# Two weight sums of a seven-product FFN on GpSimd, and three plain column pairs in place of four

## The chip, the cores and the metric

The kernel runs on one core of one Trainium2 chip. The metric is the device time of one execution in microseconds. The engines of the core are TensorE (PE, matmuls; PEld is its weight load), VectorE (DVE), ScalarE (ACT), GpSimd (POOL) and SyncE (SP). SP issues most of the DMA transfers, GpSimd those that add into their target. Each engine takes its instructions in the order in which they were written into its queue, and waits where an operand or a buffer isn't ready.

## The reference

A decoder trunk of two layers on 512 tokens of width 1024, all in float32. Each layer is an FFN, a token mixer and another FFN; the mixer of the first layer is a short gated convolution, that of the second is native sparse attention (NSA). Before each of the six a root mean square norm is scaled and shifted by a conditioning vector. So there are four FFNs; the change touches the last three. One FFN is:

```python
def swiglu(h, w_in, w_out):
    g, u = jnp.split(h @ w_in, 2, axis=-1)
    return (jax.nn.silu(g) * u) @ w_out
```

`h` is 512 x 1024, `w_in` 1024 x 5632 (gate and up, 2816 columns each), `w_out` 2816 x 1024.

## The kernel before

**Precision.** A float32 matmul is made of three matmuls in the format fp32r. An operand is split (L176, L177): ScalarE copies it to the high half, VectorE subtracts that from the operand for the low half. `mm3` (L185 to L187) multiplies high by high, high by low and low by high into the same PSUM tile. `weights` (L189 to L202) loads a block of weights into a tile `wraw` (L196, three buffers) and splits it into `whi` and `wlo` (three buffers each).

**Stages.** In the trace the first FFN and the convolution take the time up to about 569 us, the second FFN lies from there to about 904, the third to 1243, NSA to 1590 and the fourth, the last, to the end. The first FFN has code of its own (`ffn_first`), the other three run `ffn`, with f = 1, 2, 3.

**An FFN in `ffn`.** The 2816 columns of gate and up are 22 blocks of 128, numbered j. For each j the hidden block 128 x 512 (columns by tokens) is silu(gate) * up, kept split as `ahi`, `alo`. There are two ways to make gate and up of a block:

- A plain pair: gate and up, each as 8 blocks of the contraction by 3 matmuls for each half of the tokens (128x256 outputs), so 2 x 8 x 3 x 2 = 96 matmuls of 128x256, or half as many of 128x512.
- `seven_products` (L507 to L563): gate and up weights of the block are taken as the rows and the two halves of the contraction as the columns of a 2x2 matrix, the activations (halves of the contraction by halves of the tokens) as another, and the four results come from seven products instead of eight. Each product has 4 blocks of the contraction by 3 matmuls, so a block takes 7 x 4 x 3 = 84 matmuls of 128x256. The activations enter as quarters, four of them as sums that `quarters` makes once per FFN (their halves are `th`, `tl`). The weights enter as a11, a12 (`raw`, L525, split to `whi`, `wlo`), a22 (L526, its own tile `a22`), two differences s3, s1 in `qa` and two sums s2, s4 in `qb`. `qa` is loaded by SP (L520, L521, 128x512 each) and a DMA of GpSimd then accumulates onto it (L523, waits for both). `qb` is made by two additions of 128x512 (L527, L528) from `qa` and `raw`. Split halves: `qah`, `qal` of `qa`; `qbh`, `qbl` of a22 (128x512) and of `qb` (128x1024).

The seven products run in the order a11, a12, s3, s1, a22, s2, s4. The results are put together by VectorE (L556 to L562) and split into `ahi`, `alo`. Two products of one column block share a PSUM tile, three such tiles are used per block.

**The order of blocks.** Blocks 0 and 1 are plain pairs made while the norm is finished (`head_start`), block 2 is a plain pair whose gate weights are loaded into a place of their own, block 3 is a plain pair, and the other 18 are `seven_products`. The output projection is done in four parts, as soon as the hidden blocks of a part are there: `FOUR = ((0, 6), (6, 12), (12, 18), (18, 22))` (L31, L592). So in the first group two blocks by seven products precede the first output part, then six, six and four.

**Buffers of `qa`.** The first three come from two buffers of their own, then four places are cycled: the tiles of the activations' quarter that only plain pairs read (`hhi1`, `hlo1`), and the two own buffers (`sums`, L580 on). A quarter place can be loaded once the last plain pair has read it; the third `qa` once the first block's `qa` has been read (by its split and by L527). `raw`, `whi`, `wlo` have three buffers each, `a22` shares four buffers with other temporaries (`tmp`), `qb` has one.

**What sets the order.** The source is written block by block, and a scheduler in the framework places each instruction into its engine's queue by its own estimate of when its operands are ready, so a load of a later block may stand before or behind loads of an earlier one. The queues that result are fixed at compile time.

Of the kernel before, what the change touches and what calls it, by code (L numbers as in the profile page):

```python
# [17 lines left out]
ALU = mybir.AluOpType  # L18
# [36 lines left out]
def decoder_kernel(ctx, tc, xT, cT, ng, adaw, adab, ffi, ffo, cwi, cw, cwo,  # L55
                   nwi, nwg, pos, w1, w2, qg, kg, nwo, rb, onehot, rowok, out):
    nc = tc.nc
# [20 lines left out]
    def psum(name, tag="mm"):  # L78
        tag = next(six) if tag == "mm" else {"pr": "o"}.get(tag, tag)
        return ps.tile([P, T], F32, name=name, tag=tag, bufs=2)  # L80
# [4 lines left out]
    def tmp(name, n=T, tag="t"):  # L85
        bufs, size = TAGS[tag]
        return tp.tile([P, n], F32, name=name, tag=tag, padded_shape=[P, size], bufs=bufs)
# [87 lines left out]
    def split(src, hi, lo):  # L175
        nc.scalar.activation(hi, src, AF.Copy)  # L176
        nc.vector.tensor_tensor(lo, src, hi, ALU.subtract)  # L177
# [6 lines left out]
    def mm3(o, sh, sl, mh, ml, first, last):  # L184
        nc.tensor.matmul(o, sh, mh, start=first, stop=False)  # L185
        nc.tensor.matmul(o, sh, ml, start=False, stop=False)  # L186
        nc.tensor.matmul(o, sl, mh, start=False, stop=last)  # L187
# [16 lines left out]
    def project(o, w, wc, h, ks, first, last, a=0, b=T):  # L204
        c = slice(wc * P, (wc + 1) * P)
        for n, (kw, k) in enumerate(ks):
            mm3(o, w[0][:, kw, c], w[1][:, kw, c], h[0][k][:, a:b], h[1][k][:, a:b],
                first and n == 0, last and n == len(ks) - 1)
# [194 lines left out]
    def ffn_in(f, j, c, own=None):  # L403
        return weights(ffi[f, j, c], KD, P, own)
# [6 lines left out]
    class Hidden:  # L411
# [4 lines left out]
        def keep(self, af):  # L416
            hi = self.fa.tile([P, T], F32R, name="ahi", tag="a")
            lo = self.fa.tile([P, T], F32R, name="alo", tag="a")
            split(af, hi, lo)
            self.hi.append(hi)  # L420
            self.lo.append(lo)
# [21 lines left out]
    def pair(f, j, h, own=None, gate=None, halves=False):  # L443
        gu = []
        for c in range(2):
            w = gate if gate and not c else ffn_in(f, j, c, own if c else None)
            o = psum("gu")
            for a, b in HALVES if gate or halves else ((0, T),):
                project(o[:, a:b], w, 0, h, [(k, k) for k in range(KD)], True, True, a, b)
            gu.append(o)  # L450
        return gu
# [47 lines left out]
    def ffn(s, f, nrm, nxt, w0, ahead):  # L499
        with ExitStack() as es:  # L500
            hp = pool(es, "hp", 1)
            hid = Hidden(es, 12)
            keep = hid.keep
            nj = 2
# [3 lines left out]
            def seven_products(j):  # L508
                QT = KD * P // 2
                quart = lambda c, k: ffi[f, j, c].rearrange("p k n -> p (k n)")[:, k * QT:(k + 1) * QT]  # L510
                raw = wp.tile([P, 2, QT], F32, name="wraw", tag="wraw", bufs=3)
                whi = wp.tile([P, 2, QT], F32R, name="whi", tag="whi", bufs=3)
                wlo = wp.tile([P, 2, QT], F32R, name="wlo", tag="wlo", bufs=3)
                qa = next(sums)()
                a22 = tmp("a22")
                qb = swa.tile([P, 2, QT], F32, name="qb")
                ah_, al_ = (sw.tile([P, 2, QT], F32R, name=f"qa{e}", bufs=2) for e in "hl")
                bh_, bl_ = (sw.tile([P, 3, QT], F32R, name=f"qb{e}") for e in "hl")
                e = sw.tile([P, 4, HT], F32, name="e")
                nc.sync.dma_start(qa[:, 0], quart(0, 0))  # L520
                nc.sync.dma_start(qa[:, 1], quart(1, 1))  # L521
                a21 = quart(1, 0)
                nc.gpsimd.dma_start(qa, bass.AP(tensor=a21.tensor, offset=a21.offset, ap=[a21.ap[0], [0, 2], a21.ap[1]]),  # L523
                                    accum_op=ALU.add)
                nc.sync.dma_start(raw.rearrange("p a b -> p (a b)"), ffi[f, j, 0].rearrange("p k n -> p (k n)"))  # L525
                nc.sync.dma_start(a22, quart(1, 1))  # L526
                nc.vector.tensor_tensor(qb[:, 0], qa[:, 1], raw[:, 0], ALU.add)  # L527
                nc.vector.tensor_tensor(qb[:, 1], qb[:, 0], raw[:, 1], ALU.add)  # L528
                split(raw, whi, wlo)
                split(qa, ah_, al_)  # L530
                split(a22, bh_[:, 0], bl_[:, 0])
                split(qb, bh_[:, 1:3], bl_[:, 1:3])

                def product(o, w, b):
                    for i in range(KD // 2):
                        c = slice(i * P, (i + 1) * P)
                        mh, ml = b(i)
                        mm3(o, w[0][:, c], w[1][:, c], mh, ml, i == 0, i == KD // 2 - 1)

                a11, a12 = [(whi[:, i], wlo[:, i]) for i in range(2)]  # L540
                s3, s1 = [(ah_[:, i], al_[:, i]) for i in range(2)]
                a22, s2, s4 = [(bh_[:, i], bl_[:, i]) for i in range(3)]
                t1, t2, t3, t4 = nrm.blocks
                lo, hi = slice(0, HT), slice(HT, T)
                ox, oy, oz = psum("gu"), psum("gu"), psum("gu")
                both = lambda o: o.rearrange("p (a b) -> p a b", a=2)
                product(oy[:, lo], a11, nrm.quarter(0, 0))
                p1 = tmp("p1", HT, "xr")
                with tc.high_priority():
                    nc.scalar.activation(p1, oy[:, lo], AF.Copy)  # L550
                product(ox[:, lo], a12, nrm.quarter(1, 0))
                product(oy[:, hi], s3, t3)
                product(oy[:, lo], s1, t1)
                product(oz[:, hi], a22, t4)
                product(ox[:, hi], s2, t2)
                nc.vector.tensor_tensor(e[:, 0:2], both(ox), p1[:, None].to_broadcast([P, 2, HT]), ALU.add)  # L556
                nc.vector.tensor_tensor(e[:, 2], oy[:, hi], e[:, 1], ALU.add)
                nc.vector.tensor_tensor(e[:, 1:4:2], oy[:, None, lo].to_broadcast([P, 2, HT]), e[:, 1:3], ALU.add)
                product(oz[:, lo], s4, nrm.quarter(1, 1))
                nc.vector.tensor_tensor(e[:, 1:3], both(oz), e[:, 1:3], ALU.add)  # L560
                nc.scalar.activation(e[:, 0:2], e[:, 0:2], AF.Silu)
                nc.vector.scalar_tensor_tensor(e[:, 0:2], e[:, 0:2], -1.0, e[:, 2:4], op0=ALU.mult, op1=ALU.mult)  # L562
                keep(e[:, 0:2].rearrange("p a b -> p (a b)"))  # L563
# [5 lines left out]
            with ExitStack() as tf_es:  # L569
                nrm.alloc_seven(hp, pool(tf_es, "tf", 1))  # L570
                h = nrm.hi, nrm.lo
# [15 lines left out]
            shift(sw, 64)  # L587
            for j in range(nj + 1):
                hid.activate(os[2 * j], os[2 * j + 1])
            hid.activate(*pair(f, nj + 1, h, halves=True))  # L590
            nj += 2
            for p, (j0, j1) in enumerate(FOUR):  # L592
                for j in range(max(j0, nj), j1):
                    seven_products(j)
                n = j1 - j0
                a = (hid.hi[j0:j1], hid.lo[j0:j1])
                if p < len(FOUR) - 1:
                    outputs(range(KD), lambda d: ffn_out(f, d, 1, j0, j1), a, n,
                            lambda d, o: nc.vector.scalar_tensor_tensor(x[d], o, mod(s, 2, d), x[d], op0=ALU.mult, op1=ALU.add))  # L599
# [4 lines left out]
            for i, d in enumerate(range(0, KD, 2)):  # L604
                if i < 2:
                    ws.append(ffn_out(f, d, 2, j0, j1))
                else:
                    t = (2, 0)[i - 2]
                    to = [tt.tile([P, KD // 2, HT], F32R, name=f"t{e}{t}").rearrange("p a b -> p (a b)") for e in "hl"]
                    raw = swa.tile([P, 2, KD * P // 2], F32, name="qa", bufs=2).rearrange("p a b -> p (a b)")  # L610
# [660 lines left out]
    ada_es.close()  # L1271
    nrm, nxt = nxt, Norm(3)
    w = ffn(2, 1, nrm, nxt, w, ffn_ahead(2))
    nrm, nxt = nxt, Norm(4)
    w = ffn(3, 2, nrm, nxt, w, lambda: nsa_in(4))
    nrm, nxt = nxt, Norm(5)
    w = nsa(4, nrm, nxt, w, ffn_ahead(3))
    ffn(5, 3, nxt, None, w, None)


# [73 lines left out]
```

## Time and profile before

| what | value |
|---|---|
| median of 3 runs | 1951.38 us (1949.58 to 1952.29) |
| profiled execution | 1950.53 us |
| its span, first to last instruction | 1948.8 us |
| mean granted TensorE clock | 0.999 |
| second FFN, 569 to 904 us | PE busy 334.94, VectorE 251.91, GpSimd 24.08 |
| third FFN, 904 to 1243 us | PE busy 338.77, VectorE 257.55, GpSimd 22.84 |
| NSA, 1243 to 1590 us | PE busy 329.08, VectorE 278.57, GpSimd 109.56 |
| last FFN, 1590 to 1949 us | PE busy 351.52, VectorE 256.07, GpSimd 19.25 |
| first block by seven products starts on PE at | 619.81, 959.19, 1650.05 us |

The profile is one execution on the core. A row of a timeline has the start in us from the span's first instruction, the duration in us, the engine, the line of the kernel, the operation, what it writes and reads, the shapes, and how many were merged (`x2`); in brackets stands how long the engine sat idle before it and what it waited for. SPq is SP's queue. A row of the grouped view ends with the busy time, the mean of one in ns, and the idle time ahead of it. A row of the chain of waits has the start, the length and what was waited for or running. Matmuls overlap: one that is shown with 0.28 us is followed by the next 0.11 us later, so their starts and not their durations are what adds up.

### The profile page before, as it was taken

The page shows a single profiled execution, that of the slowest core. Times are in us where ns is not written, and L with a number is a line of the kernel's source. Part 1 is how long each engine was busy: PE and PEld are TensorE (multiplying, and loading weights), DVE is VectorE, ACT ScalarE, POOL GpSimd, SP SyncE. Part 2 cuts the span into 40 slices and gives each one's busy share as a digit, 9 for nine tenths or more (in the row PEclk, how much of TensorE's full clock was granted, in tenths as well). Part 3 has the DMA queues.
Part 4 walks back from the last instruction along what each step waited for, and adds up shares of the span by engine and source line. Part 5 has one row for each costly group of instructions (what it writes and reads, how often), then busy time and mean ns, then how long its engine had stood idle before and what let it go on. Part 6 is the DMA issues. An engine that isn't in the chain of part 4 may idle for free.

```text
span 1948.8 us, 32285 instructions
## 1 busy us (share of the span) xinstructions
PE 1906.6 (98%) x12600; PEld 1727.2 (89%) x12600; DVE 1459.3 (75%) x2519; ACT 869.7 (45%) x1401; POOL 191.8 (10%) x294
## 2 busy tenths in 40 slices
PE   6999999999999999999999999999999899999999
PEld 4888888898899898999989899999888789898989
DVE  8878878774468596878858686885787987685965
ACT  4322222342236353434635343466788855353532
POOL 0000000100010000000000000002434420000000
PEclk9999999999999999999999999999999999999999
DMA  8889989532145564534556453236333423665621
GB/s 318 311 316 325 330 305 326 202 98 98 67 125 164 149 173 136 156 104 130 165 144 175 142 149 114 68 130 163 89 76 70 115 77 114 181 164 143 173 82 66
DMA packets 113671, 313.42 MB, mean 161 GB/s; under 512 B 13996, under 2 KB 14268, under 8 KB 113517
## 3 DMA queue, kind: packets, MB, share of 16 engines
q1 hardware_dynamic: 96208, 273.88, 41.4%
q0 software_dynamic: 17216, 37.33, 11.2%
q8 instruction: 99, 1.62, 0.3%
q14 instruction: 56, 0.45, 0.1%
q10 hardware_dynamic: 92, 0.14, 0.0%
HBM read 308.15 MB, written 3.15 MB: 160 GB/s over the span
## 4 chain that ended last, share of the span: by engine, by line
PE 87%; DVE 5%; ACT 4%; issue 2%; DMA 1%; SPq 0%; POOL 0%; DVEq 0%; ACTq 0%
PE gu L187 13%; PE gu L186 13%; PE gu L185 13%; PE y L185 8%; PE y L186 8%; PE y L187 7%; PE hs L186 2%; PE hs L187 2%; PE hs L185 2%; PE cv L186 2%; PE cv L185 2%; PE cv L187 2%; PE ty L186 2%; PE ty L185 2%; PE ty L187 2%
## 5 line engine op out<-in xcount | busy, mean ns | idle before, releaser
L176 ACT ACTIVATE whi<-wraw 128x1024 fp32r<-128x1024 f32 (+2 forms) x274 | 270.8, 996 | 490.8 <-PE y L186 198.6
L177 DVE TENSOR_TENSOR wlo<-wraw,whi 128x1024 fp32r<-128x1024 f32 (+2 forms) x274 | 312.7, 1146 | 59.8 <-ACT whi L176 57.9
L186 PE MATMUL gu<-hlo,whi 128*128 128x256 f32 (+1 forms) x880 | 278.2, 316 | 0.0
L185 PE MATMUL gu<-hhi,whi 128*128 128x256 f32 (+1 forms) x880 | 278.0, 316 | 0.0
L187 PE MATMUL gu<-hhi,wlo 128*128 128x256 f32 (+1 forms) x880 | 277.4, 315 | 0.0
L186 PE MATMUL y<-alo,whi 128*128 128x512 f32 x587 | 229.1, 390 | 0.0
L185 PE MATMUL y<-ahi,whi 128*128 128x512 f32 x587 | 229.0, 390 | 0.0
L187 PE MATMUL y<-ahi,wlo 128*128 128x512 f32 x587 | 228.9, 390 | 0.0
L131 DVE CUSTOM_DVE_ANT_0 adaraw<-adaraw,cond 128x1024 f32<-128x1024 f32 x144 | 174.0, 1223 | 44.0 <-DMA adaraw<-in_adaw 41.8
L185 PEld LDWEIGHTS gu<-hhi,whi 128*128 128x128 f32 x880 | 165.2, 188 | 12.9
L187 PEld LDWEIGHTS gu<-hhi,wlo 128*128 128x128 f32 x880 | 165.2, 188 | 12.3
L186 PEld LDWEIGHTS gu<-hlo,whi 128*128 128x128 f32 x880 | 165.2, 188 | 12.0
L523 POOL DMA_DIRECT2D qa<-in_ffi x54 | 65.1, 1205 | 794.5 <-DMA qa<-in_ffi 297.5
L187 PEld LDWEIGHTS y<-ahi,wlo 128*128 128x128 f32 x587 | 110.2, 188 | 23.6
L186 PEld LDWEIGHTS y<-alo,whi 128*128 128x128 f32 x587 | 110.2, 188 | 23.3 <-DVE alo L177 0.4
L185 PEld LDWEIGHTS y<-ahi,whi 128*128 128x128 f32 x587 | 110.2, 188 | 23.2
L599 DVE SCALAR_TENSOR_TENSOR x<-y,mods,x 128x512 f32<-128x512 f32 x72 | 53.4, 750 | 93.2 <-PE y L187 93.1
L185 PE MATMUL gu<-th,qbh 128*128 128x256 f32 x432 | 119.5, 277 | 1.1 <-ACT qbh L176 1.1
L187 PE MATMUL gu<-th,qbl 128*128 128x256 f32 x432 | 119.6, 277 | 0.5 <-DVE qbl L177 0.5
L186 PE MATMUL gu<-tl,qbh 128*128 128x256 f32 x432 | 119.3, 276 | 0.0
L185 PE MATMUL gu<-th,qah 128*128 128x256 f32 x432 | 119.2, 276 | 0.0
L186 PE MATMUL gu<-tl,qah 128*128 128x256 f32 x432 | 119.2, 276 | 0.0
(314 smaller groups left out, 5066.4 us busy)
## 6 DMA issues: line engine op xcount, KB each, us to landing
adaraw<-in_adaw SPq DMA_DIRECT2D x144, 512.0 KB, 6.3
wraw<-in_ffi SPq DMA_DIRECT2D x122, 512.0 KB, 4.0
qa<-in_ffi SPq DMA_DIRECT2D x108, 256.0 KB, 4.1
qa<-in_ffi POOLq DMA_DIRECT2D x54, 512.0 KB, 6.8
wraw<-in_ffo SPq DMA_DIRECT2D x72, 384.0 KB, 4.2
a<-in_ffi SPq DMA_DIRECT2D x54, 256.0 KB, 4.4
wraw<-in_cwi SPq DMA_DIRECT2D x24, 512.0 KB, 3.3
wraw<-in_nwi SPq DMA_DIRECT2D x20, 512.0 KB, 4.2
```

What stands on the lines that cost most here:

```text
L131: nc.vector.tensor_tensor_reduce(out=raw, in0=raw, in1=cond, scale=1.0, scalar=0.0, op0=ALU.mult, op1=ALU.add, accum_out=m)
L176: nc.scalar.activation(hi, src, AF.Copy)
L177: nc.vector.tensor_tensor(lo, src, hi, ALU.subtract)
L185: nc.tensor.matmul(o, sh, mh, start=first, stop=False)
L186: nc.tensor.matmul(o, sh, ml, start=False, stop=False)
L187: nc.tensor.matmul(o, sl, mh, start=False, stop=last)
L523: nc.gpsimd.dma_start(qa, bass.AP(tensor=a21.tensor, offset=a21.offset, ap=[a21.ap[0], [0, 2], a21.ap[1]]), accum_op=ALU.add)
L599: lambda d, o: nc.vector.scalar_tensor_tensor(x[d], o, mod(s, 2, d), x[d], op0=ALU.mult, op1=ALU.add))
```

## The change

Two edits. The two additions that make `qb` go from VectorE to GpSimd. And block 3 is made by `seven_products` instead of as a plain pair, so that three blocks are plain and 19 by seven products in each of the three FFNs. The lines behind the removed one are one lower in the changed kernel.

```diff
@@ -524,8 +524,8 @@
                 nc.sync.dma_start(raw.rearrange("p a b -> p (a b)"), ffi[f, j, 0].rearrange("p k n -> p (k n)"))
                 nc.sync.dma_start(a22, quart(1, 1))
-                nc.vector.tensor_tensor(qb[:, 0], qa[:, 1], raw[:, 0], ALU.add)
-                nc.vector.tensor_tensor(qb[:, 1], qb[:, 0], raw[:, 1], ALU.add)
+                nc.gpsimd.tensor_tensor(qb[:, 0], qa[:, 1], raw[:, 0], ALU.add)
+                nc.gpsimd.tensor_tensor(qb[:, 1], qb[:, 0], raw[:, 1], ALU.add)
                 split(raw, whi, wlo)
@@ -587,8 +587,7 @@
             shift(sw, 64)
             for j in range(nj + 1):
                 hid.activate(os[2 * j], os[2 * j + 1])
-            hid.activate(*pair(f, nj + 1, h, halves=True))
-            nj += 2
+            nj += 1
             for p, (j0, j1) in enumerate(FOUR):
                 for j in range(max(j0, nj), j1):
                     seven_products(j)
```

Two places show how the queues move. The first is SP's queue in the second FFN, from the third block's `qa` to the first a22. Before, the blocks by seven products own `qa_5181`, `qa_5306`, `qa_5639` (the third, in the first one's buffer), then `qa_5764` and `qa_5889` (the quarter places) and `qa_6014`; the first one's a22 is `a22_5182`:

```order
L196 DMA wraw_5430<-in_ffo 128x768
L520 DMA qa_5639<-in_ffi 128x512
L521 DMA qa_5639<-in_ffi 128x512
L196 DMA wraw_5437<-in_ffo 128x768
L520 DMA qa_6014<-in_ffi 128x512
L521 DMA qa_6014<-in_ffi 128x512
L196 DMA wraw_5482<-in_ffo 128x768
L520 DMA qa_5889<-in_ffi 128x512
L520 DMA qa_5764<-in_ffi 128x512
L526 DMA a22_5182<-in_ffi 128x512
L526 DMA a22_5307<-in_ffi 128x512
```

In the changed kernel the first is `qa_5063` with `a22_5064`, the third `qa_5313`, those in the quarter places `qa_5646` and `qa_5771`:

```order
L525 DMA wraw_5310<-in_ffi 128x1024
L196 DMA wraw_5437<-in_ffo 128x768
L520 DMA qa_5771<-in_ffi 128x512
L520 DMA qa_5313<-in_ffi 128x512
L521 DMA qa_5313<-in_ffi 128x512
L520 DMA qa_5646<-in_ffi 128x512
L526 DMA a22_5064<-in_ffi 128x512
L526 DMA a22_5189<-in_ffi 128x512
L526 DMA a22_5314<-in_ffi 128x512
```

Both loads of the third block's `qa` now stand between a quarter load and the first a22, where before only the two quarter loads stood right ahead of it. In the last FFN the order is the same, in the third the last of the four L520/L521 stands behind the a22.

The second place is GpSimd's queue in the same FFN, at the first blocks of the second group. Before it holds the accumulating loads alone:

```order
L523 DMA qa_6139<-in_ffi 128x2x512
L523 DMA qa_6264<-in_ffi 128x2x512
L523 DMA qa_6597<-in_ffi 128x2x512
L523 DMA qa_6722<-in_ffi 128x2x512
L523 DMA qa_6847<-in_ffi 128x2x512
```

Now the sums stand between them:

```order
L527 TENSOR_TENSOR qb_5898<-qa_5896,wraw_5893 128x512
L528 TENSOR_TENSOR qb_5898<-qb_5898,wraw_5893 128x512
L523 DMA qa_6604<-in_ffi 128x2x512
L527 TENSOR_TENSOR qb_6023<-qa_6021,wraw_6018 128x512
L528 TENSOR_TENSOR qb_6023<-qb_6023,wraw_6018 128x512
L523 DMA qa_6729<-in_ffi 128x2x512
L527 TENSOR_TENSOR qb_6148<-qa_6146,wraw_6143 128x512
L528 TENSOR_TENSOR qb_6148<-qb_6148,wraw_6143 128x512
L523 DMA qa_6854<-in_ffi 128x2x512
```

The two sums of a block are followed by the accumulating load of the block four further on, and the next block's sums stand behind that load.

## The prediction

> **What bounds the kernel now.** I read the page's engine shares and its chain first, then the profile's tables by window, the timelines of the three FFNs and, where TensorE stops, the chain of waits.
>
> ```profile
> PE 1906.6 (98%) x12600; PEld 1727.2 (89%) x12600; DVE 1459.3 (75%) x2519; ACT 869.7 (45%) x1401; POOL 191.8 (10%) x294
> PE 87%; DVE 5%; ACT 4%; issue 2%; DMA 1%; SPq 0%; POOL 0%; DVEq 0%; ACTq 0%
> ```
>
> TensorE is busy for 98% of the span and makes 87% of the chain. VectorE's 75% says little, since the FFNs load it more than the rest. So here are five column blocks made by seven products ("blocks" from here on), in a row in the second FFN, one window each:
>
> ```profile
> core 0: us, PE busy (x) PEld busy (x) DVE busy (x) ACT busy (x) POOL busy (x), PEclk, DMA share, GB/s
> 681.61:691.13 9.52, 9.52 (x87) 9.52 (x85) 8.91 (x12) 5.15 (x7) 0.89 (x1) 1.00 0.42 132
> ...
> sum 47.60, PE 47.60 PEld 47.60 DVE 42.83 ACT 25.39 POOL 4.81; mean PE 9.52 PEld 9.52 DVE 8.57 ACT 5.08 POOL 0.96
> ```
>
> PE is busy for all 9.52 us of each block and its clock is granted in full. VectorE is second at 8.57 to 8.91, GpSimd has a tenth. In the stream a matmul starts every 0.113 us:
>
> ```profile
> 691.13 0.28 PE L185 MATMUL gu<-hhi,whi 128*128 128x256 f32 x1
> 691.24 0.28 PE L186 MATMUL gu<-hlo,whi 128*128 128x256 f32 x1
> 691.35 0.28 PE L187 MATMUL gu<-hhi,wlo 128*128 128x256 f32 x1
> ```
>
> 84 starts at 9.52/84 = 0.1133 us fill the window exactly. So here the end is set by the number of matmuls, as long as their operands are there.
>
> **Where TensorE does stop.** Only at the first block of each of the three FFNs, which waits for its a22 (L526). The chain of waits in the last FFN, that in the third, and PE in the last:
>
> ```profile
> 1649.70 6.39 DMA a<-in_ffi
> 1656.11 0.64 ACT qbh L176
> ...
> 958.76 5.24 DMA a<-in_ffi
> 964.02 0.64 ACT qbh L176
> ...
> 1655.37 0.28 PE L187 MATMUL gu<-th,qal 128*128 128x256 f32 x1
> 1656.80 0.39 PE L185 MATMUL gu<-th,qbh 128*128 128x256 f32 x1 [1.15 <-ACT qbh L176]
> 1657.52 0.39 PE L187 MATMUL gu<-th,qbl 128*128 128x256 f32 x1 [0.23 <-DVE qbl L177]
> ```
>
> From 1655.37 to 1656.80 are 1.43 us where 0.11 would do, so 1.31 are lost; the next two starts take 0.72 for 0.23, and 0.1 goes behind them: 1.9 us. The other two FFNs have the same place:
>
> ```profile
> 964.51 0.28 PE L187 MATMUL gu<-th,qal 128*128 128x256 f32 x1
> 964.71 0.39 PE L185 MATMUL gu<-th,qbh 128*128 128x256 f32 x1
> 965.44 0.39 PE L187 MATMUL gu<-th,qbl 128*128 128x256 f32 x1 [0.23 <-DVE qbl L177]
> ...
> 619.38 2.12 SPq L526 DMA_DIRECT2D a<-in_ffi  x3
> ...
> 624.14 0.63 ACT L176 ACTIVATE qbh<-a 128x512 fp32r<-128x512 f32 x1 [2.39 <-DMA a<-in_ffi]
> ```
>
> From 964.51 to 965.44 three starts take 0.93 us for 0.34, and with 0.1 behind them 0.7 us are lost in the third FFN. In the second the high half begins 4.76 us after the issue, and only 0.2 us are lost. The a22 product is the fifth of seven, so TensorE reaches it 4 x 1.36 = 5.44 us after its first matmul (1655.37 + 0.11 - 5.44 = 1650.04, and likewise 959.18 and 619.81). The loads were issued 0.35, 0.42 and 0.43 us before these starts. Landing takes 4.8 to 6.4 us and the split 0.69, so this load has no reserve at all.
>
> **The change, part by part.**
>
> *One pair becomes a block.* A pair is 2 x 8 x 3 x 2 = 96 matmuls of 128x256, seven products are 7 x 4 x 3 = 84. 12 x 0.1133 = 1.36 us per FFN, 3 x 1.36 = **-4.08 us** if nothing else moves.
>
> *The cover of the first a22 goes.* The pair that goes was also 10.88 us of TensorE work under which VectorE finished the split of the activations and SP got through its queue. The first block now starts 10.88 us earlier: 608.93, 948.31 and 1639.17. On SP its a22 stood behind two loads that waited for nothing but the last pair:
>
> ```profile
> 618.53 0.80 SPq L520 DMA_DIRECT2D qa<-in_ffi  x2
> ...
> 603.57 1.06 ACT L176 ACTIVATE th<-hfull 128x1024 fp32r<-128x1024 f32 x1 [1.77 <-PE gu L186]
> ...
> 605.24 1.22 DVE L177 TENSOR_TENSOR tl<-hfull,th 128x1024 fp32r<-128x1024 f32 x1
> 607.59 1.23 DVE L177 TENSOR_TENSOR qal<-qa,qah 128x1024 fp32r<-128x1024 f32 x1 [1.13 <-ACT qah L176]
> ...
> 608.84 0.33 SPq L520 DMA_DIRECT2D qa<-in_ffi  x1
> 609.22 0.43 SPq L521 DMA_DIRECT2D qa<-in_ffi  x1
> ...
> 947.24 2.35 DVE L177 TENSOR_TENSOR qal<-qa,qah 128x1024 fp32r<-128x1024 f32 x2
> ```
>
> The L520 and L521 at 608.84 fill the third block's qa in an own buffer, which waits for the first block's qal (608.82). Before, that was ten microseconds ahead of the first a22; now it stands in front of it, with one quarter load ahead of it and, in the second and last FFN, another behind it. The qal follows tl (through qah on ScalarE), and tl's th waits for the gate's matmuls, which do not move: th ends at 604.63, and tl stood behind the two sums until 605.24. With these gone it starts 0.6 earlier and qal ends at 608.23; L520 608.3, L521 608.7, L520 609.1, a22 at 609.5. That is 0.57 after the block's start, where it was 0.43 before it: 1.0 late. In the last FFN the same count gives 1639.7, 0.9 late. In the third FFN the first qal ended at 948.4 (the last row holds two) and may come up to 0.8 earlier; there is one load fewer behind it, so its a22 goes out 948.5 to 949.3, which is 0.6 to 1.4 late: I take 1.0. Sum **+2.9 us** (2.5 to 3.3), all of it lost, since there was no reserve.
>
> The bytes ahead grow too, from two loads of 256 KB to four. Bounds: nothing, and what 512 KB take at 330 GB/s, the page's highest slice, 1.5 us each (the second row is L520's landing):
>
> ```profile
> GB/s 318 311 316 325 330 305 326 202 98 98 67 125 164 149 173 136 156 104 130 165 144 175 142 149 114 68 130 163 89 76 70 115 77 114 181 164 143 173 82 66
> DMA to landing us min/median/max: 2.8/4.1/6.2
> ```
>
> The four issues take some 1.2 us, in which 400 KB drain at that rate; the remaining 110 KB are 0.35 us. I take **+1.05** for three (0 to 4.5).
>
> *The sums on GpSimd.* It has only eight adds of this size in the trace, with the VectorE work beside them:
>
> ```profile
> L254 POOL TENSOR_TENSOR nacc<-nacc,sq 128x512 f32<-128x512 f32 x8 | 13.0, 1620 | 542.4 <-ACT sq L252 542.4
> L527 DVE TENSOR_TENSOR qb<-qa,wraw 128x512 f32<-128x512 f32 x54 | 37.0, 685 | 0.0
> 367.00 3.31 DVE L177 TENSOR_TENSOR wlo<-wraw,whi 128x1024 fp32r<-128x1024 f32 x2
> 367.83 1.54 POOL L254 TENSOR_TENSOR nacc<-nacc,sq 128x512 f32<-128x512 f32 x1 [363.56 <-ACT sq L252]
> 551.89 2.36 DVE L177 TENSOR_TENSOR wlo<-wraw,whi 128x1024 fp32r<-128x1024 f32 x2 [0.16 <-ACT whi L176]
> 553.46 1.93 POOL L254 TENSOR_TENSOR nacc<-nacc,sq 128x512 f32<-128x512 f32 x1 [4.64 <-ACT sq L252]
> ```
>
> An add is 1.62 us there and 0.685 on VectorE, and they hold each other up: two wlo take 2.36 us undisturbed and 3.31 when an add falls on them, 0.95 more; the add that starts at 553.46 takes 1.93, and counted from the end of the wlo at 554.25 it is 1.14. So an add costs VectorE between nothing and 0.95. Per block VectorE gives up two pitches of 0.60 = 1.2 us and may get back 2 x 0.95 = 1.9: its 8.91 becomes 7.7 to 9.6, against 9.52. At the far end it slips 0.1 us per block, 0.6 over a group of six, and here is what that eats:
>
> ```profile
> 693.14 1.21 DVE L177 TENSOR_TENSOR qbl<-qb,qbh 128x1024 fp32r<-128x1024 f32 x1
> 694.88 0.68 DVE L527 TENSOR_TENSOR qb<-qa,wraw 128x512 f32<-128x512 f32 x1
> 697.22 0.68 DVE L528 TENSOR_TENSOR qb<-qb,wraw 128x512 f32<-128x512 f32 x1
> ```
>
> The qbl ends at 694.35 and is first wanted by the sixth of the seven products, at 691.13 + 5 x 1.36 = 697.93: 3.6 us to spare. So I cost this at **0** (0 to +1 per group were the slip five times as large). The cover is TensorE's queue; without it each add would cost up to 0.95. Nothing is gained either, as VectorE isn't what TensorE waits for.
>
> The Trainium skill ("SBUF — State Buffer", Who interferes with whom) has the same as an exclusive lock: a VectorE instruction with two SBUF inputs and a GpSimd instruction that reads SBUF block each other fully. The rows agree, 3.31 against 2.36. Its "GPSIMD Engine Reference" (3.1) speaks against the change, with GpSimd's add 1.96 times as long as VectorE's; here it is 1620/685 = 2.4. By the page's ratio an add would be an estimated 1.34 us and GpSimd's queue (next) a little shorter; by the rows 1.62. The forecast is the same by both.
>
> The sums also enter GpSimd's queue, between the accumulating loads L523:
>
> ```profile
> L523 POOL DMA_DIRECT2D qa<-in_ffi x54 | 65.1, 1205 | 794.5 <-DMA qa<-in_ffi 297.5
> L176 ACT ACTIVATE whi<-wraw 128x1024 fp32r<-128x1024 f32 (+2 forms) x274 | 270.8, 996 | 490.8 <-PE y L186 198.6
> ```
>
> L523 takes 1.2 us of GpSimd, a high half 1.0 of ScalarE. That queue runs in order: the sums of block n, L523 of block n+4, the sums of n+1. L523 waits for loads that SP may issue only when the sum of n has freed their buffer. One turn is 2 x 1.62 for the adds, 0.8 for SP's two issues, 4.1 landing, 1.2: 9.3 us, with both adds held up (1.93) 10.0. Against 9.52 this slips 0 to 0.5 a turn, over four dense turns of a group at most 2.0. The sum, done at 697.90, has 4.8 us to the qbl that reads it, at 693.14 + 9.52 = 702.66, and that one 3.6 more: 8.4, less 1.0 for the high half between them, 7.4 to spare. **0** again.
>
> *Sum.* -4.08 + 2.9 + 1.05 = -0.1. The profiled run took 1950.53 us (span 1948.8 and 1.7 around it), so 1950.4 in its terms; the median of before, 1951.38, lies 0.85 above that run. So I forecast **1951.2 us**: no change. The own range of this case, from 2.5 and 0 to 3.3 and 4.5 with the runs' own +-1.3, is 1948.5 to 1954.5.
>
> **The rivals.**
>
> *The cover holds.* If SP gets past the own buffer's loads earlier, or the first a22 lands within 5.44 - 0.57 - 0.69 = 4.2 us, the full 4.08 stay: 1951.38 - 4.08 = 1947.3, 1946 if the old 2.7 us of stalls shrink too. For it: the second FFN's landing of 4.8 us. Against it: the wait for qal in front of the load on the same queue.
>
> *GpSimd's loop becomes the bound*, the slower side. Slack is 7.4 us a group, at four turns 1.85 us a turn. It decides when a turn lasts over 11.4 us, a landing of 5.5 us in place of 4.1 with both adds held up. For it: single loads take up to 6.2. Against it: the median of 4.1. At a mean of 5.8 a turn is 11.7 and a group loses 4 x (11.66 - 9.52) - 7.4 = 1.2 us; with two dense groups in each of three FFNs that is 7 us: 1958.
>
> *VectorE held up by the lock.* By the rows above it loses at most 0.1 a block. If each sum also met GpSimd's L523 and held three neighbours instead of two, 8.91 - 1.2 + 2.85 = 10.6 would be 1.1 above 9.52, and 57 blocks would lose 57 x 1.1 = 63 us less 3.6 in each of twelve groups, 20: 1971. No row shows an add that blocks twice, so this has a small chance.
>
> **How the numbers follow.** Forecast 0.55, cover holds 0.2, GpSimd's loop 0.2, lock 0.05. 0.2% is 3.9 us, about what a measurement of this kernel can tell from no change, so faster means below 1947.5: most of the cover case, 0.17. Slower means above 1955.3: the lock, most of the loop and the forecast's upper edge, 0.23. The same: 0.60. The range leaves out the lock and the ends of the other two: 1946.5 to 1957.
>
> **What would show it.** Right: 9.52 us per block in the middle of the FFNs; the first a22 of each FFN issued after the block's first matmul; before the a22 product a gap about 1.3 us longer than now, in each of the three; L527 and L528 on GpSimd at 1.2 to 1.9 us; wlo and qal now and then near 2 us; VectorE below 9.5 a block. Wrong: gaps at the start no longer than now (cover), or PE waiting for qbh or qbl in the middle of a group with GpSimd's sum just before it (loop). The stage between the third and last FFN is not touched; it should take as long as before within a microsecond.

## The result and the profile after

The changed kernel takes 1967.18 us (8 runs, 1960.90 to 1973.94) against 1951.58 us before: 1.0081 times as long, 95% interval 1.0062 to 1.0100. Forecast was 1951.2. Its runs also spread over 13 us, where those of before spread over 3. The profiled execution took 1965.06 us, its span is 1963.3, 14.5 more than before. One of the ten runs of the kernel called "four pairs, late sums" below was slow, 2110.70 us at a granted clock of 0.853, and the ratios leave it out (median 1951.30 us with it, 1951.10 without).

The engine shares of the page show what was changed, GpSimd twice as busy, but not where the time went. VectorE lost 90 instructions and is busier:

```profile
PE 1908.5 (97%) x12564; PEld 1729.5 (88%) x12564; DVE 1483.3 (76%) x2429; ACT 872.1 (44%) x1410; POOL 393.3 (20%) x411
...
PE 83%; DVE 6%; ACT 4%; DMA 2%; issue 2%; SPq 1%; POOL 0%; DVEq 0%; ACTq 0%; POOLq 0%
```

So I cut the three FFNs where TensorE's output changes: the head (the norm and the first plain pairs), the first group of blocks up to its output projection, and the later groups. Lengths in us, worked out from the starts of the matmuls (a first group starts with the plain pairs of block 2 and, where it is one, block 3):

| | heads | first groups | full groups |
|---|---|---|---|
| before | 23.1, 23.0, 25.6 | 41.3, 41.8, 43.2 | 57.2 each |
| after | 26.7, 24.4, 24.2 | 43.8, 47.9, 45.8 | 57.2 each |

The three heads became 3.6 us longer together and the first groups 11.2, although these have 3 x 1.36 us less to compute. The full groups did not move at all. The same group of six blocks in windows, before and after (columns as in the prediction's table of windows):

```profile
672.00:729.20 57.20, 57.20 (x505) 57.20 (x504) 48.37 (x64) 28.91 (x39) 4.81 (x4) 1.00 0.64 165
```

```profile
678.00:735.30 57.30, 57.30 (x506) 57.27 (x505) 50.14 (x57) 28.62 (x39) 19.83 (x13) 1.00 0.65 166
```

There the sums work as the prediction reckoned: TensorE is full in both, GpSimd took the sums over, and VectorE lost the work (the eight sums of four blocks fall into this window) but got 1.8 us more busy time, held up by them. The loss lies at the starts. TensorE's rows with a wait, in the first two blocks of each FFN of the changed kernel:

```profile
619.25 0.38 PE L185 MATMUL gu<-th,qbh 128*128 128x256 f32 x1 [0.86 <-ACT qbh L176]
627.73 0.39 PE L185 MATMUL gu<-th,qah 128*128 128x256 f32 x1 [0.89 <-ACT p L550]
962.86 0.38 PE L185 MATMUL gu<-th,qbh 128*128 128x256 f32 x1 [1.45 <-ACT qbh L176]
974.27 0.41 PE L185 MATMUL gu<-th,qah 128*128 128x256 f32 x1 [2.14 <-ACT p L550]
1657.54 0.39 PE L185 MATMUL gu<-th,qbh 128*128 128x256 f32 x1 [0.66 <-ACT qbh L176]
1667.84 0.58 PE L185 MATMUL gu<-th,qah 128*128 128x256 f32 x1 [2.67 <-ACT p L550]
```

The waits for qbh are the late a22 that was forecast. Those for `p`, ScalarE's copy of the block's first product (L550), were not. What ScalarE did ahead of that copy in the last FFN:

```profile
1656.86 0.63 ACT L176 ACTIVATE qbh<-a 128x512 fp32r<-128x512 f32 x1 [1.93 <-DMA a<-in_ffi]
1665.00 1.06 ACT L176 ACTIVATE qah<-qa 128x1024 fp32r<-128x1024 f32 x1 [7.51 <-DMA a<-in_ffi]
1665.96 0.61 ACT L176 ACTIVATE qbh<-a 128x512 fp32r<-128x512 f32 x1
1666.48 1.04 ACT L176 ACTIVATE qbh<-qb 128x1024 fp32r<-128x1024 f32 x1
1667.43 0.36 ACT L550 ACTIVATE p<-gu 128x256 f32<-128x256 f32 x1
```

The qah at 1665.00 is the third block's. ScalarE waits 7.5 us for its load, and the copy of the second block stands behind it, with TensorE behind the copy. A third place is the head of the second FFN, first GpSimd and then VectorE in the changed kernel, and the last row the same step of VectorE before:

```profile
582.25 1.72 POOL L527 TENSOR_TENSOR qb<-qa,wraw 128x512 f32<-128x512 f32 x1
584.04 1.27 POOL L528 TENSOR_TENSOR qb<-qb,wraw 128x512 f32<-128x512 f32 x1
...
581.46 2.60 DVE L278 TENSOR_SCALAR dg<-ident,rs_r 128x128 f32<-128x128 f32 x2
...
581.17 0.56 DVE L278 TENSOR_SCALAR dg<-ident,rs_r 128x128 f32<-128x128 f32 x2
```

The two dg, the last step of the norm, take 2.60 us where they took 0.56 before. TensorE waits for them, and then runs slowly for a while (two windows of the changed kernel, then the second one before; the third column from the end is the granted clock):

```profile
582.00:586.00 4.00, 1.92 (x13) 1.84 (x13) 3.21 (x4) 0.64 (x2) 3.24 (x3) 0.92 0.92 210
586.00:590.00 4.00, 4.00 (x25) 4.00 (x25) 3.92 (x11) 4.00 (x9) 0.00 (x0) 0.65 0.06 10
...
586.00:590.00 4.00, 4.00 (x37) 4.00 (x37) 3.92 (x9) 4.00 (x9) 0.00 (x0) 1.00 0.02 4
```

25 matmuls in 4 us, where before there were 37.

### The profile page after: what moved, and what is told of

Read it like the earlier page. It is cut to its first block, busy times and chain, and to the rows that moved or that the text cites. A ratio compares the mean times of both kernels' runs of the same rounds, so it can differ in the third digit from the quotient of the medians.

```text
span 1963.3 us, 32307 instructions
## 1 busy us (share of the span) xinstructions
PE 1908.5 (97%) x12564; PEld 1729.5 (88%) x12564; DVE 1483.3 (76%) x2429; ACT 872.1 (44%) x1410; POOL 393.3 (20%) x411
## 4 chain that ended last, share of the span: by engine, by line
PE 83%; DVE 6%; ACT 4%; DMA 2%; issue 2%; SPq 1%; POOL 0%; DVEq 0%; ACTq 0%; POOLq 0%
PE gu L185 12%; PE gu L186 12%; PE gu L187 12%; PE y L185 7%; PE y L186 7%; PE y L187 7%; PE hs L186 2%; PE hs L187 2%; PE hs L185 2%; PE cv L186 2%; PE cv L185 2%; PE cv L187 2%; PE ty L186 2%; PE ty L185 2%; PE ty L187 2%
## 5 line engine op out<-in xcount | busy, mean ns | idle before, releaser
L177 DVE TENSOR_TENSOR wlo<-wraw,whi 128x1024 fp32r<-128x1024 f32 (+2 forms) x271 | 347.9, 1289 | 58.7 <-ACT whi L176 55.4
L186 PE MATMUL gu<-hlo,whi 128*128 128x256 f32 (+1 forms) x808 | 258.4, 320 | 0.0
L185 PE MATMUL gu<-hhi,whi 128*128 128x256 f32 (+1 forms) x808 | 258.2, 320 | 0.0
L187 PE MATMUL gu<-hhi,wlo 128*128 128x256 f32 (+1 forms) x808 | 257.6, 319 | 0.0
L527 POOL TENSOR_TENSOR qb<-qa,wraw 128x512 f32<-128x512 f32 x57 | 95.5, 1675 | 488.8 <-DVE qbl L177 268.1
L185 PEld LDWEIGHTS gu<-hhi,whi 128*128 128x128 f32 x808 | 151.7, 188 | 12.9
L187 PEld LDWEIGHTS gu<-hhi,wlo 128*128 128x128 f32 x808 | 151.7, 188 | 12.3
L186 PEld LDWEIGHTS gu<-hlo,whi 128*128 128x128 f32 x808 | 151.6, 188 | 12.0
L185 PE MATMUL gu<-th,qah 128*128 128x256 f32 x456 | 128.0, 281 | 6.0 <-ACT p L550 6.0
L185 PEld LDWEIGHTS y<-ahi,whi 128*128 128x128 f32 x587 | 110.2, 188 | 23.2
L187 PE MATMUL gu<-th,qal 128*128 128x256 f32 x456 | 127.2, 279 | 0.0
```

The lines of the kernel that those rows point to most:

```text
L527: nc.gpsimd.tensor_tensor(qb[:, 0], qa[:, 1], raw[:, 0], ALU.add)
```

## The experiments

Each ratio is to the kernel before, run beside it on the same chip, with its 95% interval; medians of different rows come from different chips, so rows are compared by their ratios. The table gives group lengths as above, from one profiled execution each.

| | ratio | heads | first groups | full groups |
|---|---|---|---|---|
| sums only | 1.0085 (1.0068 to 1.0103) | 23.2, 23.0, 24.3 | 47.8, 49.7, 48.4 | 57.2 |
| pairs only | 1.0100 (1.0077 to 1.0124) | 23.0, 22.9, 24.2 | 46.7, 49.8, 45.4 | 57.2 |
| first sums on VectorE | 1.0086 (1.0067 to 1.0105) | 23.0, 22.9, 24.2 | 48.4, 47.0, 48.1 | 57.2 |
| first group on VectorE | 1.0096 (1.0081 to 1.0111) | 23.0, 22.8, 27.1 | 44.8, 49.7, 47.0 | 57.2, one 57.5 |
| four pairs, late sums | 0.9999 (0.9989 to 1.0008) | 23.0, 22.9, 24.2 | 42.1, 41.7, 42.5 | 57.2 |
| half accumulate | 1.0022 (1.0013 to 1.0031) | 23.0, 22.9, 24.2 | 42.0, 47.6, 45.8 | 57.2 |
| pairs, p first | 1.0004 (0.9988 to 1.0019) | 23.0, 23.0, 25.6 | 43.7, 44.8, 41.8 | 57.2 |
| three orders | 1.0054 (1.0039 to 1.0069) | 23.0, 22.8, 25.7 | 41.3, 41.4, 41.7 | 59.1 |
| gap of 384 | 1.0084 (1.0069 to 1.0099) | 23.1, 22.9, 24.3 | 43.2, 42.3, 42.6 | 59.1 |
| three orders, moved back | 1.0086 (1.0069 to 1.0102) | 23.1, 22.9, 25.5 | 41.0, 42.8, 42.3 | 59.6 |
| orders, no tile | 0.9971 (0.9961 to 0.9980) | 23.0, 22.9, 27.2 | 40.9, 40.9, 41.1 | 57.2 |
| first sum on GpSimd | 0.9986 (0.9976 to 0.9995) | 27.8, 24.1, 24.2 | 40.2, 40.9, 40.0 | 57.2 |
| a22's low half first | 0.9960 (0.9946 to 0.9973) | 23.0, 22.9, 25.5 | 40.5, 39.8, 40.0 | 57.2 |
| and late sums on GpSimd | 0.9952 (0.9939 to 0.9964) | 23.0, 22.8, 24.2 | 40.5, 39.8, 40.2 | 57.2 |
| whole change, mended | 1.0088 (1.0074 to 1.0102) | 27.7, 24.4, 27.1 | 46.6, 46.4, 44.7 | 57.2 |

### Each part alone

Sums only: the two additions go to GpSimd, the fourth pair stays.

```diff
-                nc.vector.tensor_tensor(qb[:, 0], qa[:, 1], raw[:, 0], ALU.add)
+                nc.gpsimd.tensor_tensor(qb[:, 0], qa[:, 1], raw[:, 0], ALU.add)
```

> The sums on GpSimd, but four plain pairs as before. Theory (the changed kernel's 15.6 us all lie at the starts of the FFNs, where the missing pair no longer covers the first blocks' weights, and at the head where GpSimd's first sum falls on VectorE's norm): with the pair back the cover is back, and the first block's raw weights land after the norm, so 0 to +3 us against before. Rival 1 (the sums as such cost it: port and queue of GpSimd in all blocks): nearly the whole +15.6 us, and with the fourth pair's 4.08 us on top up to +20. Groups of six blocks take 57.2 us by the theory, over 58 by rival 1.

Pairs only: the additions stay on VectorE, block 3 is made by seven products.

```diff
-            hid.activate(*pair(f, nj + 1, h, halves=True))
-            nj += 2
+            nj += 1
```

> Three plain pairs, but the sums on VectorE as before. Theory: no collision at the head, yet the first a22 still late (+0.9, +1.6, -0.5 us in the changed kernel's three FFNs) and the second block still held by the first product's copy p, which stands in ScalarE's queue behind the third block's qah (about 1.2, 2.4, 3.1 us there), less 4.08 us, plus 0 to 4 us where TensorE's clock drops after a wait: +2 to +8 us against before. Rival 2 (GpSimd's sums delay the third block's accumulating load and so cause the wait for p): that wait goes, -3 to +1 us.

Measured 1967.62 and 1969.41 us: each part alone costs as much as both. No expectation held. The sums alone were to cost 0 to +3 us and cost 17, but not by rival 1, since the full groups stay at 57.2 us. The pairs alone were to cost +2 to +8 and cost 19, and rival 2 fell too, since the wait for `p` is there with the sums on VectorE. The two kernels lose at different places, and the first groups' waits tell them apart (TensorE in the second FFN; the first row is the sums-only kernel, the second the pairs-only kernel):

```profile
629.14 0.39 PE L185 MATMUL gu<-th,qbh 128*128 128x256 f32 x1 [4.30 <-ACT qbh L176]
```

```profile
626.59 0.58 PE L185 MATMUL gu<-th,qah 128*128 128x256 f32 x1 [3.48 <-ACT p L550]
```

With the pairs alone it is the copy `p`. Its chain of waits starts at the third block's accumulating load:

```profile
613.24 10.36 DMA qa<-in_ffi
...
624.71 1.56 ACT qbh L176 x2
626.26 0.28 ACT p L550
```

With the sums alone it is the first a22. It is issued at 619.27, as in the kernel before (619.38), and yet its chain of waits has

```profile
619.27 9.16 DMA a<-in_ffi
```

where it took 4.8. What differs is GpSimd's queue. Its two L523 of that time, before and then in the sums-only kernel:

```profile
612.74 1.19 POOL L523 DMA_DIRECT2D qa<-in_ffi  x1 [31.06 <-DMA qa<-in_ffi]
620.73 1.19 POOL L523 DMA_DIRECT2D qa<-in_ffi  x1 [6.80 <-DMA qa<-in_ffi]
```

```profile
609.30 2.22 POOL L527 TENSOR_TENSOR qb<-qa,wraw 128x512 f32<-128x512 f32 x1 [2.43 <-DVE qbl L177]
...
613.71 1.18 POOL L523 DMA_DIRECT2D qa<-in_ffi  x1
615.86 1.19 POOL L523 DMA_DIRECT2D qa<-in_ffi  x1 [0.97 <-DMA qa<-in_ffi]
```

And the window from 616 to 620 us, in the same order (the last two columns are the DMA engines' busy share and GB/s):

```profile
616.00:620.00 4.00, 4.00 (x38) 4.00 (x37) 0.77 (x1) 0.11 (x1) 0.00 (x0) 1.00 1.08 293
```

```profile
616.00:620.00 4.00, 4.00 (x37) 4.00 (x37) 0.70 (x2) 0.68 (x1) 1.05 (x1) 1.00 0.92 119
```

The first of the two L523 is the third block's. The second block's sums wait until qbl has read the only `qb`, this L523 stands behind them and goes out 1.0 us later than before. The second one, by the order of the queues the sixth block's, goes out 4.9 us earlier. Its buffer is the second block's, and SP may load it once that block's first sum (L527) has read it (VectorE's sum and SP's load before, then SP's load in the sums-only kernel, where GpSimd's sum at 609.30 ends at 611.52):

```profile
613.34 0.69 DVE L527 TENSOR_TENSOR qb<-qa,wraw 128x512 f32<-128x512 f32 x1
...
614.05 0.33 SPq L520 DMA_DIRECT2D qa<-in_ffi  x1
...
611.55 0.33 SPq L520 DMA_DIRECT2D qa<-in_ffi  x1
```

So two accumulating loads of 512 KB are under way when the a22 is issued. In that window the DMA engines are nearly as busy but move 119 GB/s for 293.

### Where the two collide

First sums on VectorE, and first group on VectorE: the changed kernel with `adder = nc.vector if j == 3 else nc.gpsimd`, and the same with `j < 6`.

> The changed kernel with the sums of the first block of each FFN (j = 3) back on VectorE, all others on GpSimd. Theory: only the collision with the norm at the heads goes (2.2 + 1.4 + 1.4 us of waits, and the clock drop of 1.5 us behind the longest): 1959 to 1962 us, 5 to 8 below the changed kernel. If the collision is not a cause: within 2 us of the changed kernel's 1967.

> The changed kernel with the sums of the first group's three blocks (j = 3 to 5) on VectorE, those of the other 16 blocks of each FFN on GpSimd. Theory: GpSimd's sums cost nothing in the full groups, so this takes the time of the pairs-only kernel within 1.5 us. Rival 1 (the sums cost in every block): over 3 us more than the pairs-only kernel.

1968.06 and 1968.89 us. The heads of the second and third FFN are back at 23 us, so the collision is gone there, but the total isn't: the first groups lost as much again (6.0 us; TensorE's waits for the a22 and for `p` are longer there, and no run shows why), and in the last FFN VectorE now waited in the middle of the norm for the sum's operand (3.2 us in the pairs-only kernel too, ahead of what the table counts as head). The first expectation failed. The second held: no more than the pairs-only kernel, so GpSimd's sums in the later 16 blocks cost nothing.

Four pairs, late sums: the sums-only kernel with the first group's on VectorE. Half accumulate: the sums-only kernel, with the L523 of j = 6 to 9 cut to one of its two halves (the half left out makes the output differ).

```diff
+                if FOUR[0][1] <= j < FOUR[0][1] + 4:
+                    nc.gpsimd.dma_start(qa[:, 0], a21, accum_op=ALU.add)
```

> Four plain pairs as before; the sums on VectorE in each FFN's first group (j = 4 and 5), on GpSimd in the other 16 blocks. Theory A (the sums-only kernel loses its 17 us at the first a22 alone: GpSimd's two sums push the third block's accumulating load on, two such loads then run together with the a22, which lands in 9.2 us in place of 4.8): the queues at the start are as before, so 1949 to 1953 us, the time of before. Rival (GpSimd's sums cost in every block, by port or queue): 16/18 of the 17 us remain, 1963 or more.

> The sums-only kernel, in which the accumulating load of the second group's first four blocks (j = 6 to 9, those that run while the first a22 is on its way) adds only one of its two halves: 256 KB of 512 are left out in each, so the output differs. Theory A (traffic): the first a22 lands in 5 to 7 us in place of 9.2 and the three waits of 4.5, 5.6 and 4.6 us shrink to 0.5 to 2.5 each, 1953 to 1960 us. Rival (a place in a queue, not traffic, makes the a22 late): the waits stay over 4 us each, 1965 to 1970.

1951.30 us, the time of before, and 1954.52: with half the accumulated bytes 12 to 13 us of the sums' 17 are gone. The landing of the first a22 in the third and last FFN, in the sums-only kernel and then with half the bytes:

```profile
965.00 10.18 DMA a<-in_ffi
...
1662.86 9.03 DMA a<-in_ffi
...
959.66 8.50 DMA a<-in_ffi
...
1655.14 7.69 DMA a<-in_ffi
```

In the second FFN it is 5.40 us for 9.16. Of its waits at the a22 (4.5, 5.6, 4.6) 0.3, 3.5 and 2.6 are left, so the total fell in the range but two of the three waits did not; the profiled execution, 1958.21 us, is also the longest of the ten. Traffic is most of the cause, and the sums' place in GpSimd's queue, which moves two L523, makes it fall on the a22.

### Mending the start

Pairs, p first: in the pairs-only kernel the third block's high half is held behind the second block's copy. `issue_after` fixes the order on one engine's queue and adds no wait.

```diff
+                with tc.issue_after(copies[-1].ins) if j == nj0 + 2 else nullcontext():
+                    split(qa, ah_, al_)
```

> The pairs-only kernel with one order changed: ScalarE's high half of the third block's qa is queued behind the second block's copy p. Theory B (TensorE waits in the second block, 3.6, 5.9 and 3.2 us, only because p stands behind a half whose load takes 10 us): these waits go, and the clock drops behind them, 1953 to 1958 us. Rival (the second block waits for data of its own): no change, 1965 or more.

1951.57, below what was expected: 17.8 us less than pairs only by the medians, for one block's place in ScalarE's queue (the scheduler then placed some loads at the start otherwise too). The waits for `p` in the second block were a matter of order. The start is not calm yet: the ten runs spread from 1946.00 to 1958.90 us, and in the profiled one (1957.74) the third FFN has a wait of 2.2 us for the `p` of the third block.

Three orders: also a tile of its own for the first a22 and the first sums behind the second pair's product. The tile needs 64 bytes more than there are, taken from a gap of 448 that stands ahead of the pools of th, tl and qa.

> The pairs-only kernel with p first, with a tile of its own for the first block's a22 so that it is loaded with that block's other weights, and with the first block's two sums (VectorE) behind the second plain pair's product, so that VectorE doesn't wait for them in the middle of the last FFN's norm (3.3 us in the pairs-only kernel). Theory: all three waits of the start are gone, and the 4.08 us of fewer matmuls and before's own 2.7 us of waits come out: 1944 to 1948 us. If the burst of loads just moves the wait to the next operand: 1950 to 1958.

1961.70: the first groups shrank as expected, but every full group now took 59.1 us. The next kernel looks for the reason. Gap of 384: the kernel before with that number alone changed.

> The kernel before with one number changed: the gap ahead of the pool that holds th and tl is 384 bytes and not 448, so these tiles lie 64 bytes elsewhere; nothing else. Theory C (in the version with three changed orders groups of six blocks took 59.2 us for 57.2 because TensorE reads th and tl more slowly at the new address: 283 ns for 277 a matmul): groups of 59.2 us here too, and with 54 blocks at 0.33 us each 1966 to 1971 us. Rival (the groups were slowed by the changed orders or the extra tile): 1949 to 1953.

1966.81 us, as theory C had it, so 64 bytes cost 16.9 us. TensorE's matmuls of th in the kernel before, and with the gap of 384 (ns, min/median/max):

```profile
L185 PE MATMUL gu<-th,qah x432: 276/276/277, 622.5 to 1917.5; 128*128 128x256 f32 x144
```

```profile
L185 PE MATMUL gu<-th,qah x432: 280/283/283, 622.5 to 1933.6; 128*128 128x256 f32 x144
```

Three orders, moved back: the 64 bytes taken from ahead of the pool of qah and qal instead. Orders, no tile: nothing moved; SP issues the first a22 ahead of the loads of the third to sixth block. In both the first block's splits of a22 and `qb` also stand behind the last plain pair's product.

> The version with three changed orders (pairs only, own tile for the first a22, p ahead, sums behind the norm) with the gap of 448 bytes back, the 64 bytes taken from ahead of the pool of qah and qal instead, and the first block's qbl queued behind the last plain pair's product. Theory C: th and tl are back at their place, groups of 57.2 us, and with no wait at the start over 0.5 us 1942 to 1947 us. If the place of qah and qal counts as well: groups over 58 us, 1955 or more.

> As the version before it, but without a tile of its own for the first a22 and with every tile at its old address: SP's queue is held to issue the first a22 ahead of the third to sixth block's qa. Theory: the a22 is issued before the burst of loads and lands in time; no waits over 1 us at the starts, groups of 57.2 us, 1942 to 1948 us. If the burst moves the wait to later operands: 1949 to 1955.

1967.04 (full groups of 59.6: the place of qah and qal counts as well) and 1943.84 us. The second is faster than the kernel before, by 0.2 to 0.4%.

### What the sums do once the start is mended

All four build on the version with orders and no tile. The first puts the first block's two sums on GpSimd, the second puts the low half of the first a22 ahead of VectorE's work for later blocks, the third adds to that the sums on GpSimd from j = 6 on, the fourth has all sums on GpSimd.

> The version with orders and no tile of its own, with the sums of the first block of each FFN on GpSimd and all others on VectorE. Theory D (the first sum lands on VectorE's norm at the head, blocks its small operations and holds TensorE for 1.4 to 2.2 us, at times with a clock drop of 1.5 us behind it): 3 to 8 us slower than that version, 1947 to 1952. Rival (the collision was luck of that execution): within 1.5 us of it, 1942 to 1945.

> The version with orders and no tile of its own, with VectorE's low half of the first a22 put ahead of the second block's sums and the third block's split. Theory: of the waits of 1.05 and 1.33 us for that half in the third and last FFN most goes, 0.5 to 2.5 us faster, 1941 to 1944. Rival (the half waits for its data): no change.

> The version before it, with the sums on GpSimd from the seventh column block on (16 blocks of each FFN). Theory: nothing gained or lost, since TensorE bounds the full groups: within 1.5 us of it. Rival (GpSimd's sums cost in every block): 3 us or more slower.

> The whole change (three pairs, all sums on GpSimd) with the orders of the version without a tile of its own. Theory: the collision at the heads remains, and GpSimd's second block's sums push the third block's accumulating load on by 4 us, which its new place behind p hides: the first sum's kernel (m1) within 2 us, 1947 to 1953. If GpSimd's queue at the start costs on its own: over 1955.

1948.94, 1943.29, 1941.87 and 1969.75 us. The first sums alone cost 2.9 us by the ratios (0.9986 against 0.9971) and 5.1 by the medians, and they cost it at the heads (27.8 and 24.1 us for 23.0 and 22.9). Both the engine and the time differ here: the order that holds these sums behind the second plain pair's product holds VectorE, not GpSimd. Here are, in the second FFN, GpSimd's sum and one step of the norm on two columns, and last the same step in the kernel before:

```profile
581.71 1.72 POOL L530 TENSOR_TENSOR qb<-qa,wraw 128x512 f32<-128x512 f32 x1
...
581.05 2.41 DVE L224 SCALAR_TENSOR_TENSOR rs_a<-rs_q 128x2 f32<-128x2 f32 x1
...
580.58 0.16 DVE L224 SCALAR_TENSOR_TENSOR rs_a<-rs_q 128x2 f32<-128x2 f32 x1
```

The late sums gain nothing that can be told (the intervals 0.9946 to 0.9973 and 0.9939 to 0.9964 overlap). The version with the low half first is the clearest gain over the kernel before with sums on VectorE, 0.3 to 0.5%. With all sums on GpSimd the start breaks again, as the expectation's other branch had it (over 1955): the second block's sums block VectorE's split in front of the a22's low half (a pair of wlo takes 4.25 us for 2.36), and TensorE waits for that. A block later it waits for the third block's `p`, which stands behind the fourth block's qah:

```profile
616.70 4.25 DVE L177 TENSOR_TENSOR wlo<-wraw,whi 128x1024 fp32r<-128x1024 f32 x2
...
621.61 0.39 PE L187 MATMUL gu<-th,qbl 128*128 128x256 f32 x1 [2.36 <-DVE qbl L177]
...
640.08 0.39 PE L185 MATMUL gu<-th,qah 128*128 128x256 f32 x1 [2.09 <-ACT p L555]
```

Both waits stand in all three FFNs. GpSimd's sums at the start of an FFN cost on their own, with the pairs' orders mended.

## Why the prediction was wrong, point by point

**The saving of 4.08 us** was right, and it is there: once the start is mended (with the a22's low half first) the first groups take 40.5, 39.8 and 40.0 us for 41.3, 41.8 and 43.2, 6.0 us less, of which some 2 are waits of before that are gone as well.

**The first a22** was forecast 2.9 us late for its place and 1.05 for traffic, +3.95 in all. In the changed kernel its waits are 1.6, 2.2 and 1.5 us with the starts behind them, against 0.2, 0.7 and 1.9: +2.5, at the lower end of what the two terms allowed (2.5 to 7.8). The mechanism holds, the sizes less: the load goes out 0.67, 1.46 and 0.66 us behind the block's first matmul, so 4.0 us later in all for the 2.9 reckoned, and its landing, 5.1, 5.1 and 4.9 us to the high half for 4.8, 5.3 and 6.4, got no longer. That the sum comes near is partly luck, and in the last FFN the wait shrank.

**The step that failed** is "The cover of the first a22 goes". It took that load for the only thing the pair had covered. The pair covered the third block's qa as well: that load was ten microseconds ahead, I said so, and went no further than its place in front of the a22. ScalarE's queue has its high half in front of the second block's copy, so its lateness reaches TensorE a whole block before its data is needed: 1.2, 2.4 and 3.1 us in the changed kernel. The answer stood one queue further than I looked, and with the half behind that copy the pairs-only kernel falls from 1969.41 to 1951.57 us. In the trace of the changed kernel the first groups, beside the saving, lost 15.3 us: 2.5 at the a22, 6.7 at this `p`, 4.4 at half clock behind waits, 0.6 at the third block's `p`, the rest in small pieces.

**The price of a late load** was taken from the median of L520, 4.1 us, and 0.35 us for crowding. For the first a22 of the changed kernel that was near. The third block's accumulating load, which had no price, took 7.2, 9.4 and 8.8 us there from its issue to the high half; in the sums-only kernel, with two such loads under way, the a22 took 9.2.

**The sums at nothing** was right for the full groups (57.2 us before and after; with the prediction's pitch of 0.60 VectorE is held up by 1.6 us a block, (50.14 - 48.37 + 8 x 0.60)/4, within the 0 to 1.9 reckoned), and is the other step that failed, at the starts. In GpSimd's queue it was put at 0 from the slack of dense turns, but there the sums move two accumulating loads onto the first a22: alone they cost 17 us, and with the pairs' orders mended the whole change still takes 1969.75. It was wrong at the heads too. There VectorE is what TensorE waits for, and the first block's raw weights now land early enough for GpSimd to add them in the middle of the norm: 3.6 (some 1.5 of it at half clock) and 1.4 us in two heads of the changed kernel, 2.9 to 5.1 in all by the kernel with the first sum on GpSimd. I priced the sums in dense blocks alone. The last head shows no such cost: TensorE's two waits there are 1.17 and 0.74 us after and 1.14 and 0.73 before, and the table's 1.4 us less is the half clock that followed them before and not after. So "only at the first block" was not quite so either: these two waits and that stretch are in the trace of before.

**The clock** was in no term. Four stretches of 2.6 to 3.6 us in which matmuls start 0.213 us apart stand in the three FFNs of the changed kernel's trace, behind waits of 1.5 to 2.7 us, and 1.2 to 1.7 us are lost in each; one stands in that of before.

**The rivals**: the cover did not hold, GpSimd's loop never became the bound, and the lock cost nothing in the dense blocks. The sum's own range ends wrongly: 1951.38 - 4.08 + 3.3 + 4.5 + 1.3 is 1956.4, not 1954.5. The forecast of no change rested on two terms that happened to cancel, with the larger ones left out. How the loss of the changed kernel divides between pairs and sums stays open, since each alone costs as much as both. Open too is why the runs of the changed kernel spread over 13 us: only one execution of it is profiled. The clock drops could do it, since its runs at a mean clock of 0.997 took 1961 to 1965 us and those at 0.994 and 0.995 took 1969 to 1974, but no trace of the slower ones shows it.

## What to carry to other kernels

When a piece of work is taken out ahead of a start, list every load and split that ran beneath it, and for each one follow the queues on which it stands in front of something needed sooner; the engine that waits may be two queues away. Price a load in a burst by what is under way at that moment, not by its median over the kernel. An engine that is idle on average can still hold up the one in front of the bound, at the few places where that one sets the time.

## What the runs showed of the hardware

Moving a tile of TensorE's operands by 64 bytes slowed its matmuls of 128x256 from 276 to 283 ns, 57.2 to 59.1 us for a group of 504, when the pools of th, tl and qa were moved, and 57.2 to 59.6 us when that of qah and qal was.

In one window of 4 us with two accumulating loads in flight the DMA engines moved 119 GB/s at a busy share of 0.92, in the same window of the kernel before 293 at 1.08. A plain load of 256 KB behind two such loads took 9.2, 10.2 and 9.0 us for 4.8, 5.2 and 6.4, and 5.4, 8.5 and 7.7 with half their bytes.

After a wait of 2.08 us (head of the second FFN, changed kernel) matmuls started 0.213 us apart for 3.4 us, then 0.113 again. The Trainium skill ("TensorE: Matmul & The Clock Gate", Part 1) has a half clock after an idle window of about 3.4 us, on a window that runs freely. The half rate and this length agree with the trace; the wait was shorter than a window, and a pair of waits of 1.1 and 0.7 us in the head of the last FFN was followed by the half clock before and not after. In the last three FFNs of all profiled runs, 9 of the 15 waits of TensorE of 1.9 to 2.7 us were followed by it, and all 17 of 2.8 us and more. Nor is the length fixed: in the last head of the version with orders and no tile the granted clock is 0.60 and 0.54 over two windows of 4 us in a row.
